# The first stage of a two-layer streaming encoder: x loaded ahead of all else, its squares summed on TensorE, and the order of TensorE's work written down

## The chip, the cores and the metric

The kernel runs on one core of a Trainium2 chip. The metric is the device time of one execution in microseconds (us). TensorE (PE in the profile, its weight loads PEld), VectorE (DVE), ScalarE (ACT) and GpSimd (POOL) compute; SyncE (SP) and ACT issue the transfers from memory, each in its own queue and in order.

## The reference, cut to what matters

x has 256 tokens of 2048 features in 32-bit floats. Layer 0 mixes over time, layer 1 attends; each has an MLP behind it. Only the start of layer 0 changes:

```
mod = c @ w_ada[0] + b_ada[0];  sh1, sc1 = the first two of its six parts
h  = x * rsqrt(mean(x*x) + eps) * g_mix * (1 + sc1) + sh1
xx = shift(h, one token) - h
xr, xw, xk, xv, xa, xg = h + xx * mu[0..5]
v  = xv @ w_v
tanh(xw @ w1), xa @ a1, sigmoid(xg @ g1)      # narrow projections ("lora")
r  = xr @ w_r;   k = xk @ w_k                 # next stage
```

## The kernel before, in words

Features lie on the 128 partitions, so x is 16 K tiles (KT) of 128 features by 256 tokens, held in the tile `h`. Big matrix products are made from two halves of each number: ACT rounds the weights or activations to a short type (`wH`, the H of `aHL`), DVE subtracts to get the rest (`wL`, the L of `aHL`), and TensorE runs three matmuls for each block. The small products, marked fp32 in the source by plain tiles, take two matmul records each in the trace.

The first stage is `layer_a`, up to `s3.close()`. It goes over the 16 K tiles, n = 0 to 15. For each n it needs

- the modulation of these 128 features. `w_ada0` holds, for each n, four blocks of 512 KB (tile name `rawa`, six buffers); 32 matmuls with a 32-column weight (`crep`, c copied over 32 columns) make the products in four column groups of the array (line 631 before; "products" below), ACT copies them to `adat` (637), 8 matmuls with one column sum and turn them (641; "vectors" below), DVE adds the bias (646) and makes the gain (648);
- the norm `r`, from the sum over all 16 tiles of the squares of x: before, ACT squares a tile (485, 488), DVE adds it to `ss` (489), one matmul with ones sums over partitions (494), and DVE and ACT make the reciprocal root (496 to 504);
- h (705 on DVE, 707 on ACT), xx (663, POOL), and five mixes (668, DVE);
- two matmuls and two more for the narrow projections (714, 718, weights `lw`), 24 for the first half of v (722 to 724, weights `raw` from `w_v_rows`), and from n = 4 on 24 for a part of v's second half (`v_part`, 687 to 689, weights `raw` from `w_v`, result in the PSUM tile `t`).

A scheduler sets the order of each engine's instructions from the order of the source and its own estimates; `tc.issue_after(instruction)` keeps what stands in it behind that instruction in the schedule. Tiles from pools with few buffers, and the semaphores of the transfers (eight, used in turn), add waits on SP. Before, the generator `ada_blocks` issues the products of tile n+1 in two halves ahead of tile n's work (`next(adab)` in the loop), and nothing is pinned, so the scheduler puts these matmuls in pieces between others. The transfers of x are split: quarters 1 and 3 on SP ahead of `rawa`, quarters 0 and 2 on ACT behind the first constants.

After `layer_a`'s loop come four more `v_part`, then the projections and the recurrence of layer 0 and all the rest, which the change does not touch.

Of the kernel before, what the change touches and what calls it, by code (L numbers as in the profile page):

```python
# [11 lines left out]
F32 = mybir.dt.float32  # L12
# [5 lines left out]
P = 128  # L18
D = 2048
T = 256  # L20
# [306 lines left out]
class Body:  # L327
# [163 lines left out]
    def rstd(self):  # L491
        nc = self.nc
        ps = self.psm()[:, :T]
        nc.tensor.matmul(ps, self.cst("ones"), self.ss, start=True, stop=True)
# [96 lines left out]
    def layer_a(self, st, sp):  # L591
# [6 lines left out]
        with ExitStack() as s1:  # L598
# [20 lines left out]
            def ada_blocks():  # L619

                for lo in range(KT):
                    ps = self.psm().rearrange("p (i n) -> p i n", i=4)
                    for part in (1, 0):
                        raws = []
                        for a in range(KT // HK):
                            raw = pb.tile([P, HK, P], F32, tag="rawa", bufs=6, name="rawa")
                            nc.sync.dma_start(out=raw, in_=d["w_ada0"][lo, part, a])
                            raws.append(raw)
                        for kt in range(KT):
                            g = 32 * (kt % 4)  # L630
                            nc.tensor.matmul(ps[g:g + 32, part, :], crep[:, kt, :], raws[kt // HK][:, kt % HK, :],
                                             start=(part == 1 and kt < 4), stop=(part == 0 and kt >= KT - 4),
                                             tile_position=(0, g))
                        if part:
                            yield
                    t = pb.tile([P, 2, P], F32, tag="adat", bufs=1, name="adat")
                    nc.scalar.copy(t, ps[:, 0:2, :])
                    ps = self.psm()
                    for part in range(2):
                        for g in range(0, P, 32):  # L640
                            nc.tensor.matmul(ps[g:g + 32, part:part + 1], t[:, part, g:g + 32], self.col(C_32ND),
                                             start=True, stop=True, tile_position=(0, g))
                    o = slice(lo, lo + 1)
                    for part in (1, 0):
                        bias = self.ada_src(0, part)[1]
                        nc.vector.tensor_tensor(out=self.mods[(0, part)][:, o], in0=ps[:, part:part + 1],
                                                in1=bias[:, o], op=ALU.add)
                    nc.vector.scalar_tensor_tensor(out=gain[:, o], in0=self.mods[(0, 1)][:, o], scalar=1.0,
                                                   in1=self.vec("g_mix0")[:, o], op0=ALU.add, op1=ALU.mult)
                    yield  # L650
# [489 lines left out]
```

## Time and profile before

| what | before |
|---|---|
| time, median of 3 runs | 2738.26 us (2733.71 to 2740.51) |
| the profiled execution: time, span | 2732.68 us, 2730.7 us |
| mean granted clock of TensorE | 0.991 |
| busy in the span: PE, DVE, ACT, POOL | 97%, 75%, 50%, 13% |
| first h (705) starts | 26.90 us |
| last h (705) starts | 182.14 us |
| first matmul of the next stage (pj, 400) | 205.86 us |
| moved in the whole span | 662.70 MB, mean 243 GB/s |

The span runs from the first to the last instruction of the profiled execution; its own time is 1.98 us longer. In the answers of the trace each row has a start and a length in us, the engine, the source line, the operation, result <- operands, shape and count, and in brackets the idle time ahead of it and what ended it. A row with a count covers instructions that follow each other. In rows by stretches of time, each engine's busy us stand with the number of instructions, then the granted clock (PEclk, 1.00 is full), the busy share of the 16 DMA engines and GB/s.

### The profile page before, as it was taken

To read this page: it belongs to the slowest core of one execution; us is meant where nothing else is said; L and a number is where in the kernel's file an instruction comes from. 1 tells how busy PE (TensorE), PEld (TensorE's weight loads), DVE (VectorE), ACT (ScalarE), POOL (GpSimd) and SP (SyncE) were. 2 spreads that over 40 slices of the span, in tenths; PEclk is the share of its full clock that TensorE was granted. 3 is DMA by queue.
4 is the path that set the end of the run, shared out by engine and by line. 5 is a ranking of instruction groups with operands and counts; after the bars stand their busy time and mean duration, and the time that the engine had idled before them with its cause. 6 is when DMAs were issued, how large, how long until landed. Compare 5 with 4: busy or idle time off the path is not lost.

```text
span 2730.7 us, 59448 instructions
## 1 busy us (share of the span) xinstructions
PE 2645.1 (97%) x24298; PEld 2250.2 (82%) x24298; DVE 2041.8 (75%) x2986; ACT 1363.3 (50%) x2457; POOL 361.0 (13%) x480
## 2 busy tenths in 40 slices
PE   6999999999999999999999899999999999999997
PEld 5787777777889888888888888877888888888886
DVE  5568777878799687788888788899996655566554
ACT  3346555555457543345544474465465533455443
POOL 0003434443212000000000130000120000000011
PEclk9999999999999999999999999999999999999999
DMA  9866546555688688888888778988875555555553
GB/s 349 299 243 197 172 157 191 191 170 167 214 301 286 224 284 302 316 315 315 308 307 309 249 241 310 329 307 279 283 267 194 185 190 188 187 190 186 190 188 124
DMA packets 192817, 662.70 MB, mean 243 GB/s; under 512 B 21409, under 2 KB 36129, under 8 KB 192545
## 3 DMA queue, kind: packets, MB, share of 16 engines
q1 hardware_dynamic: 190480, 656.36, 70.3%
q8 instruction: 191, 3.13, 0.5%
q10 hardware_dynamic: 2064, 2.54, 0.3%
q14 instruction: 82, 0.66, 0.1%
HBM read 656.72 MB, written 2.10 MB: 241 GB/s over the span
## 4 chain that ended last, share of the span: by engine, by line
PE 77%; DVE 7%; DMA 5%; issue 2%; ACT 2%; POOL 1%; DVEq 0%; SPq 0%; POOLq 0%; ACTq 0%
PE pj L400 41%; PE pj L401 20%; DMA rawt<-w_ada 3%; DVE wL L369 2%; PE iv L106 2%; DVE acc L430 2%; PE gr L100 1%; PE pj L391 1%; PE pj L390 1%; PE pj L389 1%; PE o L389 1%; DMA rawm<-w_ada 1%; ACT wH L366 1%; PE ms L100 1%; PE chn L279 1%
## 5 line engine op out<-in xcount | busy, mean ns | idle before, releaser
L400 PE MATMUL pj<-aHL,wH 128*128 128x512 f32 x4352 | 1574.7, 402 | 4.0 <-DVE ks L962 1.2
L369 DVE TENSOR_TENSOR wL<-raw,wH 128x1024 fp32r<-128x1024 f32 x772 | 951.5, 1234 | 421.7 <-ACT wH L366 419.1
L366 ACT CAST wH<-raw 128x1024 fp32r<-128x1024 f32 x772 | 805.9, 1046 | 878.3 <-PE pj L400 767.5
L401 PE MATMUL pj<-aHL,wL 128*128 128x256 f32 x4352 | 1226.6, 282 | 4.8 <-DVE wL L369 4.4
L400 PEld LDWEIGHTS pj<-aHL,wH 128*128 128x128 f32 x4352 | 821.2, 189 | 203.0 <-issue 11.5
L401 PEld LDWEIGHTS pj<-aHL,wL 128*128 128x128 f32 x4352 | 822.5, 189 | 12.0 <-DVE wL L369 9.5
L400 PE MATMUL pj<-hHL,wH 128*128 128x512 f32 x1024 | 359.0, 394 | 0.0
L401 PE MATMUL pj<-hHL,wL 128*128 128x256 f32 x1024 | 284.2, 278 | 0.0
L489 POOL TENSOR_TENSOR ss<-ss,sq 128x256 f32<-128x256 f32 x56 | 55.2, 986 | 1477.3 <-ACT sq L488 1477.1
L400 PEld LDWEIGHTS pj<-hHL,wH 128*128 128x128 f32 x1024 | 192.0, 188 | 44.5
L430 DVE SCALAR_TENSOR_TENSOR acc<-rawm,ct,acc 128x1024 f32<-128x1024 f32 x165 | 215.3, 1305 | 10.5 <-DMA rawm<-w_ada_kv 6.3
L401 PEld LDWEIGHTS pj<-hHL,wL 128*128 128x128 f32 x1024 | 192.3, 188 | 0.0
L430 DVE SCALAR_TENSOR_TENSOR acc<-rawt,ct,acc 128x1024 f32<-128x1024 f32 x100 | 129.7, 1297 | 21.4 <-DMA rawt<-w_ada 21.1
L430 DVE SCALAR_TENSOR_TENSOR acc<-raw,ct,acc 128x1024 f32<-128x1024 f32 x95 | 127.4, 1341 | 0.8 <-DMA raw<-w_ada 0.6
L389 PE MATMUL pj<-aHL,wH 128*128 128x258 f32 x384 | 112.4, 293 | 9.4 <-DVE ks L976 7.1
L391 PE MATMUL pj<-aHL,wL 128*128 128x258 f32 x384 | 111.4, 290 | 5.6 <-DVE wL L369 5.5
L390 PE MATMUL pj<-aHL,wH 128*128 128x258 f32 x384 | 111.7, 291 | 2.4 <-DVE aHL L513 2.4
L926 DVE SCALAR_TENSOR_TENSOR x<-pj,mod,x 128x256 f32<-128x256 f32 x128 | 61.7, 482 | 38.9 <-PE pj L401 37.2
L519 POOL TENSOR_TENSOR sq<-x,rstd 128x256 f32<-128x256 f32 x64 | 67.7, 1070 | 125.1 <-DVE aHL L522 70.7
L389 PEld LDWEIGHTS pj<-aHL,wH 128*128 128x128 f32 x384 | 75.1, 195 | 10.7 <-issue 7.3
L391 PEld LDWEIGHTS pj<-aHL,wL 128*128 128x128 f32 x384 | 75.9, 198 | 7.0 <-DVE wL L369 6.5
L390 PEld LDWEIGHTS pj<-aHL,wH 128*128 128x128 f32 x384 | 75.3, 196 | 3.0 <-DVE aHL L513 2.8
(255 smaller groups left out, 3026.6 us busy)
## 6 DMA issues: line engine op xcount, KB each, us to landing
raw<-w_up SPq DMA_DIRECT2D x256, 512.0 KB, 4.3
raw<-w_down SPq DMA_DIRECT2D x256, 512.0 KB, 3.9
rawm<-w_ada SPq DMA_DIRECT2D x111, 512.0 KB, 6.0
rawt<-w_ada SPq DMA_DIRECT2D x107, 512.0 KB, 4.7
raw<-w_ada SPq DMA_DIRECT2D x102, 512.0 KB, 4.2
rawa<-w_ada SPq DMA_DIRECT2D x64, 512.0 KB, 6.5
rawm<-w_ada_kv SPq DMA_DIRECT2D x64, 512.0 KB, 6.5
raw<-w_k SPq DMA_DIRECT2D x32, 512.0 KB, 4.0
```

The lines of the kernel that those rows point to most:

```text
L100: self.b.nc.tensor.matmul(o(c)[K], lhsT(c)[K], rhs(c)[K], start=True, stop=True)
L366: nc.scalar.copy(Hf, raw)
L369: eng.tensor_tensor(out=Lf, in0=raw, in1=Hf, op=ALU.subtract)
L389: nc.tensor.matmul(ps, H[:, i, :], a(kt)[:, 0, :], start=(first and kt == 0), stop=False)
L390: nc.tensor.matmul(ps, H[:, i, :], a(kt)[:, 1, :], start=False, stop=False)
L391: ins = nc.tensor.matmul(ps, L[:, i, :], a(kt)[:, 0, :], start=False, stop=(last and kt == KT - 1))
L400: nc.tensor.matmul(ps, H[:, i, :], a(kt), start=(first and kt == 0), stop=False)
L401: ins = nc.tensor.matmul(ps[:, 0, :], L[:, i, :], a(kt)[:, 0, :], start=False, stop=(last and kt == KT - 1))
L430: nc.vector.scalar_tensor_tensor(out=acc, in0=raw, scalar=ck, in1=acc, op0=ALU.mult, op1=ALU.add)
L489: (eng or nc.gpsimd).tensor_tensor(out=self.ss, in0=self.ss, in1=sq, op=ALU.add)
L519: nc.gpsimd.tensor_tensor(out=t, in0=self.x[:, n, :], in1=rstd, op=ALU.mult)
L926: nc.vector.scalar_tensor_tensor(out=x, in0=ps[:, i, :], scalar=self.mods[(layer, 5)][:, n:n + 1], in1=x, op0=ALU.mult, op1=ALU.add)
```

## The change

- The four quarters of x are all issued by SP, ahead of everything else. The constants' second part is no longer loaded at the start by ACT but by SP in the loop's second tile. There the name `first`, which held the column 133 where this part begins, has been set anew in the tile before (`first, last = n == 0, n == KT - 1`); the slice begins at column 1 and takes 1092 columns instead of 960, 546 KB instead of 480. It writes again the ones and the column of 1/32, which the vectors' matmuls read.
- The squares go alternately to ACT and DVE into four buffers (`sqa`), and each is summed by a matmul with ones into one PSUM tile: 16 such matmuls instead of 15 additions and one matmul.
- `ada_blocks` becomes `ada_load`, `ada_products` and `ada_vectors`. In tile n the products of tile n+1 come first, as one group; then the narrow projections; then the first half of v's 24 matmuls; then the vectors of tile n+1; then the second half; then `v_part`. Each of these is kept behind the last matmul issued before it (`behind()`).
- xx of the first two tiles moves from POOL to DVE.

```diff
+            for q in range(4):
+                nc.sync.dma_start(out=h[:, 4 * q:4 * q + 4, 1:T + 1], in_=d["x"][:, 4 * q:4 * q + 4, :])
             nc.scalar.dma_start(out=self.csts[:, :first], in_=d["cst"][:, :first])
-            for q in range(4):
-                (nc.sync if q % 2 else nc.scalar).dma_start(out=h[:, 4 * q:4 * q + 4, 1:T + 1],
-                                                            in_=d["x"][:, 4 * q:4 * q + 4, :])
             nc.scalar.dma_start(out=self.bada, in_=d["b_ada"])
             nc.scalar.dma_start(out=self.vecs, in_=d["vecs"])
-            nc.scalar.dma_start(out=self.csts[:, first:], in_=d["cst"][:, first:])
...
-            def ada_blocks():
...
-            adab = ada_blocks()
-            self.ss_reset()
+            def ada_load(m):
...
+                        nc.sync.dma_start(out=raw, in_=d["w_ada0"][m, part, a])
+            def ada_products(m):
+                raws = ada_load(m) if m else raws0
+                ps = self.psm().rearrange("p (i n) -> p i n", i=4)
+                for part in (1, 0):
+                    for kt in range(KT):
+                        g = 32 * (kt % 4)
+                        nc.tensor.matmul(ps[g:g + 32, part, :], crep[:, kt, :], raws[part, kt // HK][:, kt % HK, :],
...
+                nc.scalar.copy(t, ps[:, 0:2, :])
+                return ps[:, 2, :], t
+            def ada_vectors(m, sums):
...
+            raws0 = ada_load(0)
+            pss = pp.tile([P, 2, T], F32, tag="t", bufs=1, name="t")[:, 0, :]
             for n in range(KT):
-                self.ss_add(h[:, n, 1:T + 1], n, nc.vector)
-            adab_at = 2
-            for i in range(adab_at):
-                next(adab)
-            r = self.rstd()
+                sq, x = pb.tile([P, T], F32, tag="sqa", bufs=4, name="sqa"), h[:, n, 1:T + 1]
+                if n % 2:
+                    nc.vector.tensor_tensor(out=sq, in0=x, in1=x, op=ALU.mult)
+                else:
+                    nc.scalar.activation(sq, x, AF.Square)
+                nc.tensor.matmul(pss, self.cst("ones"), sq, start=(n == 0), stop=(n == KT - 1))
+            ada_vectors(0, ada_products(0))
+            r = self.rstd(pss)
             def diff(n):
-                nc.gpsimd.tensor_tensor(out=xx, in0=h[:, n, 0:T], in1=h[:, n, 1:T + 1], op=ALU.subtract)
+                (nc.gpsimd if n > 1 else nc.vector).tensor_tensor(out=xx, in0=h[:, n, 0:T], in1=h[:, n, 1:T + 1],
+                                                                  op=ALU.subtract)
+            def behind():
+                return tc.issue_after(self.last_pe())
...
             for n in range(KT):
...
-                while adab_at < min(2 * KT, 2 * n + 4):
-                    next(adab)
-                    adab_at += 1
+                if n == 1:
+                    nc.sync.dma_start(out=self.csts[:, first:], in_=d["cst"][:, first:])
+                if n + 1 < KT:
+                    with behind():
+                        sums = ada_products(n + 1)
...
+                with behind():
...                                    # the four matmuls of the narrow projections
+                for half in range(2):
+                    with behind():
+                        for i in range(4 * half, 4 * half + 4):
...                                    # three matmuls of v for each i
+                    if half == 0 and n + 1 < KT:
+                        with behind():
+                            ada_vectors(n + 1, sums)
                 if n == 3:
                     self.v_next = v_part_weight(0)
                 if n >= 4:
-                    v_part(n // 4 - 1, n % 4)
+                    with behind():
+                        v_part(n // 4 - 1, n % 4)
```

What this does to the order, at four places.

TensorE in a tile of the second half of the loop, before (m is the tile of products, v_229 to v_232 the first half of v, l_234 a narrow projection, t is `v_part`):

```order
L714 MATMUL l_233<-mix,lw_2101 96x256 x2
L631 MATMUL m<-rawa,crep 32x128 x8
L722 MATMUL v_229<-aHL,wH 128x256
...
L631 MATMUL m<-rawa,crep 32x128 x8
L718 MATMUL l_234<-mix,lw_2101 128x256 x2
L724 MATMUL v_229<-aHL,wL 128x256
L631 MATMUL m<-rawa,crep 32x128 x8
```

and now, with the last matmul of `v_part` of the tile before in its first row:

```order
L697 MATMUL t<-aHL,wL 128x256
L632 MATMUL m<-rawa,crep 32x128 x32
L725 MATMUL l_231<-mix,lw_1522 96x256 x2
L729 MATMUL l_232<-mix,lw_1522 128x256 x2
L735 MATMUL v_227<-aHL,wH 128x256
```

The 32 products stood in four pieces of 8 between other matmuls; they now stand in one row, ahead of the tile's other work.

SP's queue from the start, before:

```order
L609 DMA h<-x 128x4x256 x2
L627 DMA rawa<-w_ada 128x1024 x4
L699 DMA lw_235<-lora 128x448
L356 DMA raw<-w_v_rows 128x1024
L627 DMA rawa<-w_ada 128x1024 x4
```

and now:

```order
L609 DMA h<-x 128x4x256 x4
L623 DMA rawa<-w_ada 128x1024 x4
L707 DMA lw_233<-lora 128x448
L356 DMA raw<-w_v_rows 128x1024
L623 DMA rawa<-w_ada 128x1024 x4
```

All of x now stands ahead of the first modulation block; the rest is as it was. Further on, where the loop's second tile loads the four blocks for tile 2, SP's row is now, with the semaphores that each waits for:

```order
L623 DMA rawa<-w_ada 128x1024 [waits DMAHW6_49,PE_49]
L710 DMA csts<-cst 128x1092 [waits DMAHW7_49,PE_49]
L623 DMA rawa<-w_ada 128x1024 [waits DMAHW0_49]
L707 DMA lw_452<-lora 128x448 [waits DMAHW1_49]
L356 DMA raw<-w_v_rows 128x1024 [waits DMAHW2_49]
```

The constants have come in ahead of the fourth block for tile 2. Their wait for TensorE (PE_49) ends at its 112th matmul: 16 with ones, 32 products and 8 vectors of tile 0, 32 products of tile 1, 4 of the narrow projections, 12 of v and, last, the 8 vectors of tile 1.

ACT at the start, before:

```order
L609 DMA h<-x 128x4x256 x2
L611 DMA bada<-b_ada 128x224
L612 DMA vecs<-vecs 128x304
L613 DMA csts<-cst 128x960
L485 ACTIVATE ss<-h 128x256
L488 ACTIVATE sq<-h 128x256 x10
L637 COPY adat<-m 128x256
L488 ACTIVATE sq<-h 128x256 x4
L366 CAST wH<-raw 128x1024
L488 ACTIVATE sq<-h 128x256
L498 ACTIVATE rstd<-rv 128x256
```

and now:

```order
L611 DMA bada<-b_ada 128x224
L612 DMA vecs<-vecs 128x304
L660 ACTIVATE sqa<-h 128x256 x8
L499 ACTIVATE rstd<-rv 128x256
L500 ACTIVATE rstd<-rstd 128x256
L636 COPY adat<-m 128x256
L366 CAST wH<-raw 128x1024
```

The copy of the first modulation products and the first rounding of weights stood among the squares; both now stand behind the norm. Past the end of this stage the engines' rows are the same before and now.

More of the change, by code (lines that the diff above doesn't have):

```diff
@@ L489, in ss_add, with rstd @@
             (eng or nc.gpsimd).tensor_tensor(out=self.ss, in0=self.ss, in1=sq, op=ALU.add)
-    def rstd(self):
+    def rstd(self, ps=None):
         nc = self.nc
-        ps = self.psm()[:, :T]
-        nc.tensor.matmul(ps, self.cst("ones"), self.ss, start=True, stop=True)
+        if ps is None:
+            ps = self.psm()[:, :T]
+            nc.tensor.matmul(ps, self.cst("ones"), self.ss, start=True, stop=True)
         v = self.np.tile([P, T], F32, tag="rv", bufs=1, name="rv")
@@ L617, in layer_a @@
             gain = self.gp.tile([P, KT], F32, name="gain_g_mix0")
-            def ada_blocks():
[L621 to L650, printed above, removed]
@@ L652, in layer_a @@
-            adab = ada_blocks()
-            self.ss_reset()
-            for n in range(KT):
-                self.ss_add(h[:, n, 1:T + 1], n, nc.vector)
-            adab_at = 2
-            for i in range(adab_at):
-                next(adab)
-            r = self.rstd()
+            def ada_load(m):
+                raws = {}
+                for part in (1, 0):
+                    for a in range(KT // HK):
+                        raw = raws[part, a] = pb.tile([P, HK, P], F32, tag="rawa", bufs=6, name="rawa")
+                        nc.sync.dma_start(out=raw, in_=d["w_ada0"][m, part, a])
+                return raws
@@ new lines, in ada_products @@
+            def ada_products(m):
+                raws = ada_load(m) if m else raws0
+                ps = self.psm().rearrange("p (i n) -> p i n", i=4)
+                for part in (1, 0):
+                    for kt in range(KT):
+                        g = 32 * (kt % 4)
+                        nc.tensor.matmul(ps[g:g + 32, part, :], crep[:, kt, :], raws[part, kt // HK][:, kt % HK, :],
+                                         start=(part == 1 and kt < 4), stop=(part == 0 and kt >= KT - 4),
+                                         tile_position=(0, g))
+                t = pb.tile([P, 2, P], F32, tag="adat", bufs=1, name="adat")
+                nc.scalar.copy(t, ps[:, 0:2, :])
+                return ps[:, 2, :], t
@@ new lines, in ada_vectors @@
+            def ada_vectors(m, sums):
+                ps, t = sums
+                for part in range(2):
+                    for g in range(0, P, 32):
+                        nc.tensor.matmul(ps[g:g + 32, part:part + 1], t[:, part, g:g + 32], self.col(C_32ND),
+                                         start=True, stop=True, tile_position=(0, g))
+                o = slice(m, m + 1)
+                for part in (1, 0):
+                    bias = self.ada_src(0, part)[1]
+                    nc.vector.tensor_tensor(out=self.mods[(0, part)][:, o], in0=ps[:, part:part + 1],
+                                            in1=bias[:, o], op=ALU.add)
+                nc.vector.scalar_tensor_tensor(out=gain[:, o], in0=self.mods[(0, 1)][:, o], scalar=1.0,
+                                               in1=self.vec("g_mix0")[:, o], op0=ALU.add, op1=ALU.mult)
```

23 lines of the change are left out of this document (11 added, 12 removed).

## The prediction

> **What bounds the kernel now.** I read the page's table of busy time first, then the stretches of the first stage, then its rows in order of time.
>
> ```profile
> PE 2645.1 (97%) x24298; PEld 2250.2 (82%) x24298; DVE 2041.8 (75%) x2986; ACT 1363.3 (50%) x2457; POOL 361.0 (13%) x480
> 0.00:8.40 8.40, 0.00 (x0) 0.00 (x0) 0.50 (x2) 1.28 (x1) 0.21 (x4) 1.00 0.76 268
> 8.40:26.90 18.50, 8.50 (x146) 5.62 (x146) 9.62 (x25) 7.94 (x20) 0.00 (x0) 1.00 1.04 397
> 114.00:182.14 68.14, 67.07 (x818) 54.05 (x818) 41.85 (x91) 21.49 (x37) 5.52 (x6) 1.00 0.80 289
> ```
>
> TensorE is the bound, so only idle or ill-used TensorE time can be won. Until 26.90 us it is busy 8.50 of 18.50 us while transfers run full (1.04, 397 GB/s): a start that waits for x, the norm and the first modulation. Later it is busy 67.07 of 68.14 us, which does not say how well. The start in order of time:
>
> ```profile
> 8.43 1.08 PE L631 MATMUL m<-rawa,crep 128*32 128x128 f32 x16 [8.43 <-DMA rawa<-w_ada]
> 10.77 0.42 ACT L485 ACTIVATE ss<-h 128x256 f32<-128x256 f32 x1 [8.73 <-DMA h<-x]
> 11.09 4.49 ACT L488 ACTIVATE sq<-h 128x256 f32<-128x256 f32 x10
> 16.80 1.08 PE L631 MATMUL m<-rawa,crep 128*32 128x128 f32 x16 [2.89 <-DMA rawa<-w_ada]
> 17.95 0.37 ACT L637 COPY adat<-m 128x256 f32<-128x256 f32 x1 [2.37 <-PE m L631]
> 19.75 1.03 ACT L366 CAST wH<-raw 128x1024 fp32r<-128x1024 f32 x1
> 22.03 0.42 DVE L489 TENSOR_TENSOR ss<-ss,sq 128x256 f32<-128x256 f32 x1
> 22.59 1.19 PE L494 MATMUL m<-ss,csts 128*128 128x256 f32 x2 [3.83 <-DVE ss L489]
> 23.83 0.42 DVE L496 TENSOR_SCALAR rv<-m 128x256 f32<-128x256 f32 x1 [1.38 <-PE m L494]
> 24.31 2.76 PE L631 MATMUL m<-rawa,crep 128*32 128x128 f32 x64 [0.52 <-DVE rv L496]
> 26.90 0.49 DVE L705 SCALAR_TENSOR_TENSOR h<-h,gain_g_mix,rstd 128x256 f32<-128x256 f32 x1
> 28.24 0.31 PE L641 MATMUL m<-csts,adat 128*32 128x1 f32 x16 [1.17 <-ACT adat L637]
> 29.72 2.02 PE L714 MATMUL l<-mix,lw 128*96 128x256 f32 x4 [1.18 <-DVE mix L668]
> ```
>
> The first square waits for x until 10.77. After eleven, ACT stands at the copy of the modulation products, which came with the fourth `rawa` at 16.80, and later rounds weights at 19.75; so the last addition ends at 22.45 and h starts at 26.90.
>
> **The start.** Removed: 15 additions and those two waits in ACT's row. Added: 15 matmuls with ones. Moved: two quarters of x from ACT's queue to SP's, ahead of the modulation blocks.
>
> ```profile
> rawa<-w_ada SPq DMA_DIRECT2D x14, 512.0 KB, 7.0
> raw<-w_v_rows SPq DMA_DIRECT2D x3, 512.0 KB, 6.6
> h<-x SPq DMA_DIRECT2D x2, 512.0 KB, 4.8
> h<-x ACTq DMA_DIRECT2D x2, 512.0 KB, 10.1
> lw<-lora SPq DMA_DIRECT2D x3, 224.0 KB, 6.2
> vecs<-vecs ACTq DMA_DIRECT2D x1, 152.0 KB, 9.0
> bada<-b_ada ACTq DMA_DIRECT2D x1, 112.0 KB, 8.9
> csts<-cst ACTq DMA_DIRECT2D x1, 66.5 KB, 5.2
> 29.50:30.00 0.50, 0.28 (x1) 0.28 (x2) 0.50 (x3) 0.08 (x1) 0.00 (x0) 0.50 1.02 372
> 33.00:34.00 1.00, 1.00 (x9) 0.97 (x9) 0.67 (x1) 0.00 (x0) 1.00 (x1) 1.00 1.02 414
> 36.02 1.95 PE L631 MATMUL m<-rawa,crep 128*32 128x128 f32 x64
> 37.90 1.10 PE L714 MATMUL l<-mix,lw 128*96 128x256 f32 x4
> ```
>
> x (2.10 MB) and the small loads beside it (0.34 MB) are 2.44 MB. Before, the first `rawa` was there at 8.43 behind two quarters of x and with as much again on ACT's queue, so I put that amount at 9 us. The squares (0.42 us each, on two engines) end at about 10 and hold nothing up. The ones landed 5.2 us after an early issue on ACT's queue: about 6.4 us. From there 16 matmuls run one behind another. The same kind of product took 2.02/2 = 1.01 us at a granted clock of 0.50, and 1.10/2 = 0.55, or 0.52 from start to start, at 1.00; between 29.5 and 33 the clock needed about 3.4 us to rise. Bounds: all slow, 16.2 us, end at 22.6; all fast, 8.3, end at 14.7. I take 3.4 us slow (3.3 matmuls) and 12.7 x 0.52 = 6.6: 16.4, or 17 with some waiting for x. From the old sum's end (23.78) to h took 3.1 us: 20.1. Beside it the products of tile 0 follow the ones on TensorE (1.88 us, 36.02 to 37.90), then copy, vectors, bias, gain, about 1.5 us: 20.4. So h starts at about 20.5, **6.4 us** earlier (4 to 9).
>
> [...]
>
> Tile 0's narrow projections also wait for the products of tile 1, now pinned ahead of them. Bytes up to these: 2.44 + 2.10 + 0.75 + 2.10 = 7.39 MB. Before, 8.40 x 0.268 + 18.50 x 0.397 = 9.6 MB were through at 26.90; at 0.397 MB a us 7.39 are there at 21.4, and the products end at about 23. The mixes (h, ACT, a `wL` of 1.2 us, xx, three mixes) are ready at about 24: line 714 starts at 24 instead of 29.72. xx on DVE costs 0.42 us there and saves the hop to POOL; I cost it at nothing, since `rawa` is nearly as late; without that cover it is under 1 us in two tiles.
>
> **Tiles 1 to 4.** The constants are a new wait in SP's row: they are issued after the vectors of tile 1, at 24 + 2.1 + 1.5 = 27.6, and behind them stand the fourth block for tile 2 and all later loads. Without that, TensorE would set these tiles: 7.4 us each (below). With it, 1.08 MB land 2.7 us later at the least (by rate) and 7.0 at most (the `rawa` row); I take 4.8 (x on SP's empty queue): 32.4, products done at 33. From there transfers set the pace: 4 x 0.52 + 0.52 + 0.23 = 2.85 MB a tile, 7.2 us at 397 GB/s; with the first `raw` of `v_part`, 3.37 MB, 8.5 us. Line 714 of tile 4 then starts at 33 + 7.2 + 7.2 + 8.5 = 56, against 59.96 (row below): **4.0 us** left of the start (6 if TensorE alone sets these tiles, -1 if the waits let the clock fall, rival A).
>
> **Tiles 4 to 15.** The steady tile, some rows in order:
>
> ```profile
> 56.90 0.49 DVE L705 SCALAR_TENSOR_TENSOR h<-h,gain_g_mix,rstd 128x256 f32<-128x256 f32 x1
> 182.14 0.48 DVE L705 SCALAR_TENSOR_TENSOR h<-h,gain_g_mix,rstd 128x256 f32<-128x256 f32 x1
> 59.96 1.10 PE L714 MATMUL l<-mix,lw 128*96 128x256 f32 x4 [0.29 <-DVE mix L668]
> 151.03 1.10 PE L714 MATMUL l<-mix,lw 128*96 128x256 f32 x4
> 152.07 0.65 PE L631 MATMUL m<-rawa,crep 128*32 128x128 f32 x16
> 152.64 0.39 PE L722 MATMUL v<-aHL,wH 128*128 128x256 f32 x1
> 152.87 0.29 PE L723 MATMUL v<-aHL,wH 128*128 128x256 f32 x1
> 153.59 0.28 PE L723 MATMUL v<-aHL,wH 128*128 128x256 f32 x1
> 153.80 0.64 PE L631 MATMUL m<-rawa,crep 128*32 128x128 f32 x16
> 158.64 0.31 PE L641 MATMUL m<-csts,adat 128*32 128x1 f32 x16
> 162.47 0.67 PE l L714 x2
> ```
>
> (182.14 - 56.90)/11 = 11.39 us a tile. v matmuls follow each other after 0.12 us (six steps from 152.87 to 153.59), but the first behind a piece of products holds 0.23, and a piece starts 0.21 after the last v: each visit to the column groups costs 0.1 + 0.1 us beside its own 0.57 (152.07 to 152.64). Four pieces and the vectors: 4 x 0.57 + 0.24 + 5 x 0.2 = 3.5 us; narrow projections 4 x 0.52 = 2.1; v and `v_part` 48 x 0.119 = 5.7; sum 11.3, nearly the period. Now: products 1.88, vectors 0.24, two visits 0.4, and 2.1 + 5.7: **10.3 us** (7.4 without `v_part`). Bounds: only the shorter group, 0.4 us a tile won; or 1.3, with the wait of 0.29 ahead of 714 gone too. 11 x 1.05 = **11.5 us** (4 to 14).
>
> What is late next: from the vectors to the next narrow projections 162.47 - 158.64 = 3.83 us, and up to 2 more where a `wL` and an `aHL` come between the mixes. Behind the vectors TensorE now has 1.5 (v) + 2.9 (`v_part`) + 2.1 (products) = 6.5 us: cover by 0.7. The last tile has no products: 0.7 us lost. A tile's 3.37 MB need 8.5 us, under 10.3.
>
> **Sum:** 4.0 + 11.5 - 0.7 = 14.8 us off the profiled execution's 2732.68: 2717.9. The median of runs lies 5.6 above that execution: 2738.26 - 14.8 = 2723.5. Nothing behind the stage is reordered, so I carry the gain to the end whole.
>
> **The rivals.**
>
> A. Cold tiles. In tiles 1 to 4 TensorE waits for blocks with everything else pinned behind them. After the pause between 27.07 (24.31 + 2.76) and 29.72, with 0.31 us of work in it, the clock stood at 0.50 for 3.4 us and lost 1.7. Three such tiles lose 5: gain 9.7, 2728.6; four, 8. Against it: the waits should be about 1 us, not 2.7. [...]
>
> B. The chain of mixes binds. If DVE or ACT are so late that the cover of 0.7 us and the gain of 1 us a tile are gone, the period stays at 11.3: gain 4, 2734. For it: POOL's hop and two roundings in the chain; against: DVE's 41.85 busy of 68.14 us.
>
> C. Slower. Pinned products make every tile wait for transfers. The steady rate was 289 GB/s; were that the most that these issues give, a tile's 3.37 MB took 11.7 us, and at 270 GB/s 12.5: 11 x 1.1 = 12 us lost against 4 won, 2746. It decides below 290. Against it: 397 GB/s at the start, and a DMA share of only 0.80.
>
> **How the numbers follow.** Forecast 0.68, A 0.15, B 0.12, C 0.05. Under 0.3% (8.2 us) this kernel's time can't be told from no change. The forecast and two thirds of A are faster by more: 0.78; the rest of A, B and a little of C 0.18; C 0.04. The range takes in A and goes to 2732, short of B; at the other end stand the better bounds of tiles 1 to 4 and of the period, 6 + 14 - 0.7 = 19, or 2719, and the lower runs' distance to the median (2738.26 - 2733.71, 4 us): 2715.
>
> **What the profile would show.** Ones from about 6.4 to 17 us, halving in length on the way; h at 20 to 21; the first narrow projection at 24; the constants issued at about 28 and a pause of SP ahead of them; tile 4's narrow projections at 56; then 10.3 us a tile with 64 products in one row of 1.9 us; the next stage's first matmul at about 191. Wrong if steady products wait for `rawa`, if the clock falls below 1.00 after 25 us, if narrow projections wait for mixes in each tile, or if later stages give the gain back.

## The result and the profile after

The changed kernel takes 2724.03 us (median of 8 executions, 2715.83 to 2731.16), the kernel before 2737.45 beside it (8 executions, 2733.71 to 2740.51): ratio 0.9949, 95% interval 0.9933 to 0.9965. The profiled execution took 2723.07 us, its span is 2721.3 at a mean granted clock of 0.987 (before: 2730.7 at 0.991).

First the page's table of busy time, then stretches of the first stage (columns as before), cut at the first h (19.02), the first narrow projection (24.41) and that of tile 1 (36.55), and six steady tiles from the narrow projections of tile 4 on (59.09 to 118.55):

```profile
PE 2647.0 (97%) x24328; PEld 2265.5 (83%) x24328; DVE 2040.2 (75%) x2981; ACT 1362.1 (50%) x2449; POOL 353.2 (13%) x478
4.97:19.02 14.05, 11.71 (x116) 9.64 (x120) 5.91 (x18) 5.38 (x12) 0.00 (x0) 1.00 1.05 393
19.02:24.41 5.39, 3.32 (x65) 1.88 (x65) 5.22 (x11) 1.32 (x3) 0.00 (x0) 0.70 1.03 402
24.41:36.55 12.14, 8.93 (x117) 7.31 (x113) 5.75 (x14) 2.74 (x5) 0.00 (x0) 0.85 0.70 256
59.09:118.55 59.46, 59.46 (x820) 54.82 (x817) 40.65 (x89) 24.31 (x40) 3.69 (x6) 1.00 0.98 364
```

The table of busy time hardly moves; the stretches do. Transfers run full until 24.41, then drop to 256 GB/s while TensorE is busy 8.93 of 12.14 us at a clock of 0.85: there the constants hold SP up. (The first row's clock reads 1.00, but the pace of the ones, shown further down, shows that their first 4.6 us ran at half the speed of the rest.) The start in order of time (TensorE, DVE, SP):

```profile
6.20 9.46 PE L661 MATMUL t<-sqa,csts 128*128 128x256 f32 x32 [6.20 <-DMA csts<-cst]
15.58 1.95 PE L632 MATMUL m<-rawa,crep 128*32 128x128 f32 x64
19.02 0.49 DVE L715 SCALAR_TENSOR_TENSOR h<-h,gain_g_mix,rstd 128x256 f32<-128x256 f32 x1
22.10 1.08 PE L632 MATMUL m<-rawa,crep 128*32 128x128 f32 x16 [1.50 <-DMA rawa<-w_ada]
24.41 2.02 PE L725 MATMUL l<-mix,lw 128*96 128x256 f32 x4
18.14 1.84 SPq L623 DMA_DIRECT2D rawa<-w_ada  x3
29.80 0.33 SPq L710 DMA_DIRECT2D csts<-cst  x1
35.97 0.65 PE L632 MATMUL m<-rawa,crep 128*32 128x128 f32 x16 [3.21 <-DMA rawa<-w_ada]
59.09 1.10 PE L725 MATMUL l<-mix,lw 128*96 128x256 f32 x4
```

The first h comes 7.9 us earlier than before (26.90), the first narrow projection 5.3 (29.72), but tile 4's only 0.9 (59.96): between them stand the 9.8 us in which SP issues nothing, from 19.98 (18.14 + 1.84) to 29.80, and TensorE's wait of 3.21 us for a block issued behind the constants.

The steady tile, the last tile and the next stage:

```profile
63.18 0.49 DVE L715 SCALAR_TENSOR_TENSOR h<-h,gain_g_mix,rstd 128x256 f32<-128x256 f32 x1
108.60 1.10 PE L725 MATMUL l<-mix,lw 128*96 128x256 f32 x4
...
110.22 0.47 PE L735 MATMUL v<-aHL,wH 128*128 128x256 f32 x1
116.67 1.95 PE L632 MATMUL m<-rawa,crep 128*32 128x128 f32 x64
118.55 1.10 PE L725 MATMUL l<-mix,lw 128*96 128x256 f32 x4
162.39 0.48 DVE L715 SCALAR_TENSOR_TENSOR h<-h,gain_g_mix,rstd 128x256 f32<-128x256 f32 x1
185.61 0.40 PE L400 MATMUL pj<-aHL,wH 128*128 128x512 f32 x1
```

(162.39 - 63.18)/10 = 9.92 us a tile instead of 11.39, and nothing waits. The next stage begins at 185.61 instead of 205.86: the stage has won 20.25 us. The span is only 9.4 us shorter, and the medians lie 13.4 apart. So some of the stage's gain is lost behind it, where the change touches nothing. In the same places of the two programs the gain is 18.9 us at about 500 us, 14.4 at 620, 9.2 at 745, and 7.4 to 9.5 from there on. Two places take nearly all of that, 5.1 us at 584 and 5.3 at 702 (half of each half-clock stretch, and at the second a pause of 1.9 that the profile of the kernel before does not have). This is the first, by stretches of time, in the kernel before, in the changed one, and in a second profile of the changed one (`again`, below):

```profile
599.46:602.87 3.41, 1.95 (x11) 1.28 (x9) 3.41 (x4) 1.46 (x3) 3.41 (x3) 1.00 0.56 166
603.50:613.50 10.00, 9.91 (x123) 7.95 (x123) 6.67 (x15) 6.59 (x21) 3.02 (x9) 1.00 0.51 167
```
```profile
580.91:584.32 3.41, 1.86 (x11) 1.24 (x9) 3.41 (x5) 1.38 (x3) 3.41 (x3) 1.00 0.54 169
584.30:594.50 10.20, 9.55 (x68) 7.32 (x69) 3.72 (x9) 3.27 (x12) 3.58 (x9) 0.50 0.31 98
```
```profile
588.03:591.44 3.41, 1.97 (x22) 1.75 (x24) 1.36 (x3) 1.39 (x4) 3.01 (x6) 1.00 0.74 214
589.50:599.50 10.00, 10.00 (x125) 8.03 (x127) 6.79 (x15) 6.70 (x21) 2.88 (x8) 1.00 0.51 162
```

In each, TensorE stands idle at the same step of the recurrence. In the changed kernel's first profile the clock then stands at 0.50 for 10.2 us and 68 matmuls run where 123 run at 1.00. The idle time is the same in the three, as TensorE's rows show (kernel before, changed kernel, `again`):

```profile
603.59 0.39 PE L123 MATMUL py<-sL,bones 128*128 128x256 f32 x1 [2.18 <-POOL sL L118]
```
```profile
584.95 0.58 PE L123 MATMUL py<-sL,bones 128*128 128x256 f32 x1 [2.17 <-POOL sL L118]
```
```profile
589.47 0.39 PE L123 MATMUL py<-sL,bones 128*128 128x256 f32 x1 [2.18 <-POOL sL L118]
```

So the same pause of 2.2 us is followed by half clock in one execution and not in another of the same program. In the traces the stretches at 0.50 last 3.4, 6.8 or 10.2 us nearly everywhere (a few 13.7, as in `sl_dve` from 224.6 to 238.3), and within each of the 13 profiles here all changes of the clock lie on one grid with a step of 3.413 us: up to 2680 us 12 changes in the profile of the kernel before and 18 in the first of the changed one, each within 0.001 us of its grid.

The grid also tells the executions apart. The first rows of the three pairs above are each a step of their own profile's grid, the one with the larger part of the pause: TensorE is idle for 1.46 us of it before, 1.55 in the changed kernel (3.41 - 1.86) and 1.44 in `again`, and only the second is followed by half clock. Over the 13 profiles, between 150 and 2680 us, a step at full clock with 1.5 us or more of idle TensorE is followed by half clock in 74 of 77 cases, one with 1.4 to 1.5 in 8 of 22, and one with 0.9 to 1.4 in 3 of 100; in the profile of the kernel before and the first of the changed one alone it is 13 of 14, none of 3 and none of 15. So what follows a pause of this length goes here with how it lies on the grid, as far as a count over traces can show it; no run moved a pause to test it.

### The profile page after: what moved, and what is told of

Read it like the earlier page. It is cut to its first block, busy times and chain, and to the rows that moved or that the text cites. A ratio compares the mean times of both kernels' runs of the same rounds, so it can differ in the third digit from the quotient of the medians.

```text
span 2721.3 us, 59484 instructions
## 1 busy us (share of the span) xinstructions
PE 2647.0 (97%) x24328; PEld 2265.5 (83%) x24328; DVE 2040.2 (75%) x2981; ACT 1362.1 (50%) x2449; POOL 353.2 (13%) x478
## 3 DMA queue, kind: packets, MB, share of 16 engines
q8 instruction: 191, 3.13, 0.5%
## 4 chain that ended last, share of the span: by engine, by line
PE 80%; DVE 8%; DMA 7%; issue 2%; ACT 2%; POOL 1%; SPq 0%; DVEq 0%; ACTq 0%; POOLq 0%
PE pj L400 40%; PE pj L401 20%; DVE wL L369 3%; DMA rawt<-w_ada 2%; PE iv L106 2%; DVE acc L430 2%; PE gr L100 1%; PE pj L391 1%; PE pj L389 1%; PE pj L390 1%; DMA rawa<-w_ada 1%; PE m L632 1%; DMA raw<-w_q 1%; PE o L389 1%; ACT wH L366 1%
## 5 line engine op out<-in xcount | busy, mean ns | idle before, releaser
L400 PEld LDWEIGHTS pj<-aHL,wH 128*128 128x128 f32 x4352 | 821.9, 189 | 201.1 <-issue 10.1
L389 PE MATMUL pj<-aHL,wH 128*128 128x258 f32 x384 | 112.8, 294 | 10.2 <-DVE ks L993 7.3
L389 PEld LDWEIGHTS pj<-aHL,wH 128*128 128x128 f32 x384 | 75.4, 196 | 11.5 <-issue 7.7
```

What stands on the lines that cost most here:

```text
L389: nc.tensor.matmul(ps, H[:, i, :], a(kt)[:, 0, :], start=(first and kt == 0), stop=False)
L400: nc.tensor.matmul(ps, H[:, i, :], a(kt), start=(first and kt == 0), stop=False)
```

## Experiments

In each table, h, first and tile 4 are the starts of the first h and of the narrow projections of tiles 0 and 4, pj is the next stage's first matmul, all in us from the profile.

**The same kernel once more, and the late constants put right** (`again`, `csts960`). The second slices the constants from column 133, so that it writes nothing that TensorE reads.

```diff
-                    nc.sync.dma_start(out=self.csts[:, first:], in_=d["cst"][:, first:])
+                    nc.sync.dma_start(out=self.csts[:, CST_AT["ident"][0]:], in_=d["cst"][:, CST_AT["ident"][0]:])
```

> The changed kernel once more, nothing edited. In its first profile the first stage ended 19 us earlier, but 10 us of that were lost between 580 and 715 us, where the granted clock fell to 0.50 twice after a pause of TensorE of about 2 us that the kernel before has too, without the fall. Theory 1: whether the clock falls at such a pause is chance, not the change. Then the falls come at other pauses this time, or at none, and the span less half of the time at 0.50 stays at 2721.3 - 73.9/2 = 2684 +-3 us. Theory 2: the change's own timing brings the falls about. Then they are at the same two places (after the pauses at 582.8 and 702.0 us), and the gain at 700 us is again about 9 us against the kernel before.

> The late constants are read from column 133 on (960 columns), so that nothing that TensorE reads is written again, and SP's row has no wait for TensorE there. Theory: the pause of 3.2 us ahead of the last products for tile 2 (32.8 us) goes; SP issues the constants at about 19 instead of 29.8 us, tile 4's narrow projections start at 55 to 56 instead of 59.09 us, and the last h at 159 instead of 162.39; 3 us won. Rival: the transfers of tiles 1 to 4 are the limit anyway, tile 4 starts at 58 to 59 us, and under 1 us is won.

**The two halves of the change apart** (`order_only`, `start_only`). The first keeps the pinned order, but x on two queues, the constants on ACT at the start, the sum by ACT and DVE, and xx on POOL, as before. The second is the kernel before with x first on SP and the sum of squares on TensorE.

```diff
             for q in range(4):
-                nc.sync.dma_start(out=h[:, 4 * q:4 * q + 4, 1:T + 1], in_=d["x"][:, 4 * q:4 * q + 4, :])
+                (nc.sync if q % 2 else nc.scalar).dma_start(out=h[:, 4 * q:4 * q + 4, 1:T + 1],
+                                                            in_=d["x"][:, 4 * q:4 * q + 4, :])
...
-                nc.tensor.matmul(pss, self.cst("ones"), sq, start=(n == 0), stop=(n == KT - 1))
+                self.ss_add(h[:, n, 1:T + 1], n, nc.vector)
```

> The order of TensorE's work as in the changed kernel, but the start as before: x split over two queues, squares by ACT and added by DVE, constants at the start by ACT, xx on POOL. Theory: the order alone is worth (11.39 - 9.92) x 11 = 16 us from tile 4 to 15: a period of 9.9 us, and the last h at about 166 us against 182.14 before; 2721 by the kernel before's median of 2737.5, if later stages keep it. Rival: without the early start the first tiles are later, the pinned products wait for transfers, and no more than 10 us are won by the last h (172 or later).

> The start as in the changed kernel (x first on SP, squares summed by TensorE, xx still on POOL, constants by SP's neighbour ACT at the start), with the order of the rest left to the scheduler as before. Theory: the first narrow projections start 5 us earlier (24 to 25 us instead of 29.72) and this is carried through: last h at 177, 2732 by the kernel before's median. Rival: tiles 1 to 4 wait for transfers, tile 4's narrow projections stay at about 59 us, and the start is worth under 2 us by the last h (180 or later).

These four ran on one chip, the kernel before beside them at 2734.82 (18 executions):

| kernel | median (executions) | ratio, 95% interval | first | tile 4 | pj |
|---|---|---|---|---|---|
| again | 2723.36 (10) | 0.9959, 0.9944 to 0.9975 | 24.46 | 61.51 | 188.36 |
| csts960 | 2716.01 (5) | 0.9926, 0.9905 to 0.9947 | 24.47 | 54.94 | 181.69 |
| order_only | 2722.80 (5) | 0.9957, 0.9942 to 0.9972 | 29.69 | 60.58 | 188.16 |
| start_only | 2745.74 (8) | 1.0049, 1.0032 to 1.0066 | 23.55 | 61.20 | 206.00 |

The second profile of the changed kernel has no fall of the clock behind the pause near 588 us, but others elsewhere, one of them in the stage itself: at 35.1 us, in the wait behind the constants, which is why tile 4 comes 2.4 us later. So the falls are not bound to the change's two places (theory 2), but the sum that theory 1 named was not met either: the span less half of the time at 0.50 is 2688 us, not 2684 +-3.

In `csts960` SP's row does not stop, and the block that came at 35.97 is there when TensorE wants it:

```profile
17.94 0.43 SPq L710 DMA_DIRECT2D csts<-cst  x1
31.03 1.95 PE L632 MATMUL m<-rawa,crep 128*32 128x128 f32 x64
```

The constants are issued 11.9 us earlier, and tile 4 comes 4.15 us earlier than in the change. That is the price of the wait; 3.9 of it are left at pj. The median lies 7.35 us under that of `again`, but five executions from 2711.93 to 2730.15 do not tell how much of that is the edit's.

In `order_only` the start is that of the kernel before, and pj still comes 17.7 us earlier than 205.86: nearly all of the 20.25 belongs to the order. The new start adds 2.5 (188.16 to 185.61), and 6.5 without the wait for the constants (181.69). `start_only` has its first narrow projection 6.2 us earlier than before and nothing of it left at tile 4. Its TensorE in tiles 3 and 4:

```profile
50.82 0.67 PE L719 MATMUL l<-mix,lw 128*96 128x256 f32 x2 [1.39 <-DVE mix L673]
61.20 1.10 PE L719 MATMUL l<-mix,lw 128*96 128x256 f32 x4 [0.31 <-DVE mix L673]
```

Without the pinned order TensorE runs out of ready work and waits for the mixes. That is not all of the loss: between its first narrow projection and that of tile 4 it is idle for 3.6 us (0.3 before), and it does 4.1 us of matmuls (busy 34.1 us against 29.9) that the kernel before had done ahead of its first narrow projection. The rival, no gain from the start alone, was right in its outcome; its reason, waits for transfers, is not what the rows show. The median is even worse than before: its profile shows the stage no longer than before (206.00 against 205.86), and behind it half-clock stretches of 6.8 us at 442.6 and 13.7 us at 722.5 that the kernel before's profile lacks, each behind a pause of TensorE that no other engine ends (1.99 and 1.52 us; more on these at the end of the next section). By the mean of all executions it loses 35 us to half clock, (1 - clock) x span, where the kernel before beside it loses 26; the 4 us more that it takes are of the size of these two pauses, which is not proof.

**Who sums the squares** (`dve_sum`). x stays first on SP and the order pinned; ACT squares and DVE adds, with one matmul with ones, as before.

```diff
-                sq, x = pb.tile([P, T], F32, tag="sqa", bufs=4, name="sqa"), h[:, n, 1:T + 1]
...
-                nc.tensor.matmul(pss, self.cst("ones"), sq, start=(n == 0), stop=(n == KT - 1))
+                self.ss_add(h[:, n, 1:T + 1], n, nc.vector)
             ada_vectors(0, ada_products(0))
-            r = self.rstd(pss)
+            r = self.rstd()
```

> The changed kernel with x first on SP, but the squares all by ACT, summed by DVE and one matmul with ones, as before; the pinned order is kept. Theory: x's place in the queues makes the earlier start, and TensorE's sum is no quicker than DVE's 15 additions of 0.42 us, since its 16 matmuls took 9.46 us, the first of them at half clock, and the products of tile 0 stand behind them. Then the first h starts at 18.5 to 20.5 us (19.02 with TensorE's sum), the first narrow projection at 24 to 25, the next stage at 185 to 187, and the time is that of the changed kernel within 0.2%. Rival: TensorE's sum is what is won; then the first h starts at 22 to 24, the first narrow projection at 26 to 27, and the next stage some 2 us later than 185.61.

Measured: 2718.05 us (4 executions), ratio 0.9938 (0.9919 to 0.9956) to the kernel before at 2736.71; h at 21.89, first 24.35, tile 4 57.77, pj 185.33.

```profile
10.06 3.60 DVE L489 TENSOR_TENSOR ss<-ss,sq 128x256 f32<-128x256 f32 x7
18.01 0.67 PE L495 MATMUL m<-ss,csts 128*128 128x256 f32 x2 [0.50 <-DVE gain_g_mix L650]
21.89 0.49 DVE L710 SCALAR_TENSOR_TENSOR h<-h,gain_g_mix,rstd 128x256 f32<-128x256 f32 x1
22.67 1.03 PE L632 MATMUL m<-rawa,crep 128*32 128x128 f32 x16 [0.23 <-DMA rawa<-w_ada]
24.35 0.89 PE L720 MATMUL l<-mix,lw 128*96 128x256 f32 x3 [0.65 <-DVE mix L671]
```

The last products of tile 1 and their block, in the change:

```profile
23.40 1.08 PE L632 MATMUL m<-rawa,crep 128*32 128x128 f32 x16 [0.21 <-DMA rawa<-w_ada]
```

On h the rival was nearly right (22 to 24), on the rest the theory. DVE's sum ends at 13.66, before TensorE's (15.66), but its one matmul stands in TensorE's row behind the products and vectors of tile 0, and starts at 18.01. So h is 2.9 us late, and TensorE waits 0.65 us for a mix ahead of the first narrow projection, which it does not in the change. That this starts at 24.35 all the same is two differences that cancel: with no ones ahead of them the products of tile 0 start at 11.88 us instead of 15.58, SP has issued the four blocks for tile 1 by 14.5 instead of 17.1, and the last of them is used from 22.67 on, 0.7 us earlier. Where the norm's matmul stands in TensorE's row and when the blocks land matters; which engine adds makes no difference here that the first narrow projection or pj would show.

**What a visit to the column groups costs** (`twice_joined`, `twice_apart`). Both issue the eight vectors' matmuls of each tile a second time, into the same place. The first does it right behind the first copy, the second in a place of its own between two groups of v's matmuls.

```diff
+                    if half == 2 and n + 1 < KT:
+                        with behind():
+                            sum_up(sums)
```

> The changed kernel with the eight vectors' matmuls of each tile issued twice, the second time right behind the first. Both theories expect 8 x 0.03 us more in a tile: the steady period goes from 9.92 to about 10.15 us. It is there for the comparison with the next kernel.

> As the one before, with the same matmuls, but the second copy stands in a place of its own, between two groups of v's matmuls, so that TensorE goes to the column groups once more in each tile. Theory (each visit costs about 0.2 us, the reading on which the period of the prediction rests): the period is 0.2 us above that of the kernel before, about 10.35. Rival (a visit costs nothing, and the shorter period comes from something else, such as the projections' own matmuls or the waits ahead of them): the same period within 0.05 us. By the period of 9.92 itself, 0.4 below the 10.3 of the prediction, a visit could also cost about 0.3.

Narrow projections of tile 4 and, ten tiles on, of tile 14; joined, then apart:

```profile
58.28 1.10 PE L729 MATMUL l<-mix,lw 128*96 128x256 f32 x4
158.76 1.10 PE L729 MATMUL l<-mix,lw 128*96 128x256 f32 x4
```
```profile
59.95 0.89 PE L729 MATMUL l<-mix,lw 128*96 128x256 f32 x3
163.48 0.89 PE L729 MATMUL l<-mix,lw 128*96 128x256 f32 x3
```

The periods are 10.05 and 10.35 us (one execution each, 2721.44 and 2719.14 us; executions of one program differ by more than that). The second copy itself costs 0.13 us, and the place of its own 0.30: about 0.2 in the gaps beside it, as the prediction had read, and 0.1 in the group itself, which takes 0.24 apart and 0.13 joined. The theory's 10.35 is met only because the joined kernel came 0.10 under its forecast. So a visit has a price here, and 0.30 us is its size.

**The pauses behind the stage** (`sl_dve`, `before_sl`, `after_sl`). In the recurrence, TensorE waits for sL, a difference that POOL makes for the sums of py. One call of it goes to DVE: in `sl_dve` on top of the mended constants, in the two others on the kernel before and on the change as it is.

```diff
-        nc.gpsimd.tensor_tensor(out=L, in0=src, in1=H, op=ALU.subtract)
+        (eng or nc.gpsimd).tensor_tensor(out=L, in0=src, in1=H, op=ALU.subtract)
...
-        sq = self.parts(AF.Square, py)
+        sq = self.parts(AF.Square, py, eng=nc.vector)
```

> The changed kernel with two edits: the late constants start at column 133 again, and in the recurrence the subtraction that makes sL for the sums of py (line 118, for this one call) goes from POOL, where it took 1.70 us behind another of 1.70, to DVE. Theory (the falls of the clock between 200 and 850 us follow TensorE's pauses of about 2 us, four or five of them at py, line 123, waiting for sL): these pauses shrink below 1 us, no fall follows them, the half-clock time in that stretch is 10 to 20 us instead of 20 to 54, and the median is 5 to 10 us below the 2716.01 of the kernel with the constants alone, 2706 to 2711. Rival (falls come whatever pauses there are, or DVE, now later with its own work, makes new pauses in the same place): half-clock time and median as there, 2713 to 2719.

> The kernel before, with one edit outside the first stage: the subtraction that makes sL for the sums of py goes from POOL to DVE. It shows what that edit alone is worth, and is the base for the next kernel. Theory (the pauses at py cost their own length of about 1.7 us, five times, and now and then a fall of the clock behind them): 8 to 13 us below the kernel before, ratio 0.9952 to 0.9971, with half-clock time of 40 to 50 us a run against the 52 that 25 runs of the kernel before had in the mean. Rival (it only helped where the change had moved the recurrence to another moment): within 0.15% of the kernel before.

> The changed kernel with that edit alone (the late constants as in the change). Against the kernel before_sl on the same chip it shows what the change is worth where the pauses at py are gone from both. Theory (the stage wins 18 to 20 us up to the next stage's first matmul, and what the medians of before and after lack of that, 13.4 instead of 20, went to falls of the clock behind the pauses of the recurrence): 17 to 21 us below before_sl, a median of 2707 to 2711. Rival (the gain is lost for another reason, such as waits further on that only the changed kernel has): 9 to 14 us below before_sl, as the change was below the kernel before; 2712 to 2717.

| kernel | median (executions) | the kernel before beside it | ratio, 95% interval |
|---|---|---|---|
| sl_dve | 2706.45 (4) | 2736.71 | 0.9893, 0.9869 to 0.9917 |
| before_sl | 2727.05 (6) | 2737.18 | 0.9956, 0.9940 to 0.9972 |
| after_sl | 2709.22 (5) | 2737.18 | 0.9896, 0.9881 to 0.9911 |

Some of TensorE's longest waits between 200 and 850 us (sum, times, longest), in the changed kernel and in `sl_dve`, and the edited operation in `sl_dve`:

```profile
PE py L123 <- POOL sL L118: 7.6, 4, 2.2
PE py L292 <- issue: 1.9, 1, 1.9
```
```profile
PE iv L106 <- DVE tt L238: 4.1, 4, 2.1
```
```profile
L118 DVE TENSOR_TENSOR sL<-pt,sH x16: 412/426/829, 263.4 to 709.1; 128x256 fp32r<-128x256 f32 x16
```

The waits at py are gone, and no half clock stands between 238 and 784 us in that profile; 17.1 us are left between 200 and 850, where `csts960` had 54.6. The waits at iv remain (4.1 us in four, against 4.3 in five in the changed kernel), and 13.7 us at half clock, from 224.6 to 238.3, follow one of them. The times came as the theory said in all three (in `after_sl` by the medians). What the clock alone gave back is less than the two profiles suggest: that of `csts960` is its slowest execution, and the profile of the kernel before, with four pauses at py, has 17.1 us at half clock in this stretch too. By the mean of all executions the time lost to half clock is 22 us in `before_sl` against 29 beside it, 25 in `after_sl` against 33 in the change, and 27 in `sl_dve` against 29 in `csts960`. The edit alone wins 10.1 us without the change (`before_sl`). With the pauses gone from both, the change wins 2727.05 - 2709.22 = 17.8 us by the medians, 16.5 by the means, instead of 13.4; in its profiles the stage wins 20.20 (pj at 206.42 and 186.22). `sl_dve` is the fastest kernel of this study, 17.6 us under the change's 2724.03 (on another chip) and 30.3 under the kernel before beside it.

**The first tile's own work first** (`own_first`). As `sl_dve`, but in tile 0 the products of tile 1 stand behind the narrow projections and half of v.

```diff
+                    if half == 0 and n == 0:
+                        with behind():
+                            sums = ada_products(1, raws1)
```

> The kernel with the constants from column 133 and sL on DVE, and in tile 0 alone the products of tile 1 behind the narrow projections and the first half of v, not ahead of them. Theory (from x's arrival on the first tile waits only for the blocks of tile 1, the last of which came at 23.86, and everything behind is TensorE's own work): the first narrow projection starts at 21.5 to 22.5 us instead of 24.88, TensorE waits for no block, and the narrow projections of tile 1 start at 30.5 to 31.5 instead of 32.71, the next stage 1 to 2 us before 181.55. Rival (the pause from 17.9 us to the first narrow projection, now with no products in it, lets the clock fall for longer, or transfers bind tiles 1 to 4): the narrow projections of tile 1 at 32.3 or later, and the next stage at 181.2 or later.

```profile
22.22 2.02 PE L727 MATMUL l<-mix,lw 128*96 128x256 f32 x4 [3.61 <-DVE mix L676]
26.90 1.95 PE L632 MATMUL m<-rawa,crep 128*32 128x128 f32 x64
31.25 0.48 DVE L717 SCALAR_TENSOR_TENSOR h<-h,gain_g_mix,rstd 128x256 f32<-128x256 f32 x1
33.71 1.10 PE L727 MATMUL l<-mix,lw 128*96 128x256 f32 x4 [0.34 <-DVE mix L676]
```

The first narrow projection comes 2.7 us earlier, tile 1's 1.0 later than in `sl_dve` (32.71), pj at 183.48 instead of 181.55. The rival's outcome, but for neither of its reasons: the half-clock stretch there is shorter (3.4 us instead of 6.8), and no matmul waits for a block. What is late is the vectors of tile 1, now behind products that start at 26.90; h of tile 1 waits for them, at 31.25 instead of 29.77. Pinned ahead, the products of the next tile give the chain of h its lead. (2710.11 us, one execution.)

## Why the prediction was right, point by point

The forecast of 2723.5 us came out at 2724.03. That it lies so near is luck: the stage won 20.25 us where 14.8 was forecast, and part of it was lost behind the stage where nothing was forecast. Most of the stage's gain came in the way that was forecast, by the shorter period.

- **Ones and h.** Ones from 6.20 to 15.66 (6.4 to 16.4 or 17 forecast), h at 19.02 (20.5). ACT, which waits for every second of the ones to free a buffer, shows their pace:

```profile
9.13 0.42 ACT L660 ACTIVATE sqa<-h 128x256 f32<-128x256 f32 x1 [1.29 <-PE t L661]
10.84 0.42 ACT L660 ACTIVATE sqa<-h 128x256 f32<-128x256 f32 x1 [1.29 <-PE t L661]
12.67 0.42 ACT L660 ACTIVATE sqa<-h 128x256 f32<-128x256 f32 x1 [0.45 <-PE t L661]
13.53 0.42 ACT L660 ACTIVATE sqa<-h 128x256 f32<-128x256 f32 x1 [0.45 <-PE t L661]
```

  1.71 us for two, then 0.86: it halves, as forecast, though later (about 4.6 us after the first instead of 3.4) and to 0.43 each instead of 0.52. The 3.4 us were an estimate from one rise of the clock in the kernel before (at 0.50 from 29.43 to 32.84 us); no run shows them for a start, where these 4.6 us stood in their place. That the early start needs x's place in the queues and not TensorE's sum was not seen; `dve_sum` shows it for the first narrow projection and for pj, not for h (24.35 with x first on SP, 29.69 in `order_only` with x on two queues, both with DVE's sum). The move of xx to DVE was not run alone.
- **First narrow projection.** 24.41 (24 forecast), for the reason given: the products of tile 1, released by their blocks (the last from 23.40 on).
- **The constants.** The mechanism was right: SP waits for the vectors of tile 1. Two sizes failed. The issue came at 29.80 instead of 27.6, because the clock fell at 21.1 for 6.8 us while the products waited for blocks, and the narrow projections and the first of v ran at half speed: one of the signs that the prediction had named for being wrong (a clock below 1.00 after 25 us; it lasted to 27.9). From the issue to the block took 6.2 us (29.80 to 35.97) where 4.8 was taken from a range of 2.7 to 7.0. So tile 4 came at 59.09 instead of 56, and the **start term was 0.9 instead of 4.0 us**. From the products to tile 4 took 22.5 us (23 forecast).
- **The period.** 9.92 instead of 10.3 us: the **period term was 16 us instead of 11.5**. The visits were sized well: the working has three of them at 1.0 us in all (3 x 0.2 in the gaps, and four pieces of 0.57 against one of 1.88), `twice_apart` makes it 0.90, and the rows show 0.93 (from each start to the next, in the mean of ten tiles from tile 4 on: products 2.30 before and 1.88 now, v's first half 3.76 and 3.24). The term that failed is the narrow projections: 4 x 0.52 = 2.1 was set for both orders, where they took 1.86 before and 1.62 now (108.60 to 110.22). That the old sum closed at 11.3 all the same was luck, since it had no term for waits, which took 0.31 us a tile, mostly for mixes; they are gone too. 0.93 + 0.24 + 0.31 is the 1.47 us won in a tile.
- **Last tile.** The loss of 0.7 us did not come: behind the last `v_part` TensorE waits 0.17 us for a mix. Instead 3.3 us were won that the sum has no term for. In the new order the products of tile n+1 stand ahead of the narrow projections of tile n, so tile 4's mark lies behind the products of tile 5, and the last step, from tile 14 to 15 (158.30 to 166.24), has none in it: 7.94 us, 2.0 less than a period. These 2.0 are work done before the mark at tile 4, and belong to the start, which by work was worth 2.9 us. The other 1.3 came between tile 15's narrow projections and pj, where a wait of 0.87 us for v is gone. So the stage's gain of 20.25 us is 0.9, 11 x 1.46 = 16.1, and 3.3.
- **"Nothing behind the stage is reordered, so I carry the gain to the end whole."** This step failed, and with it came another of the signs, that later stages give the gain back. By the mean of all executions here whose clock is on record (36 of before, 18 of the change) span times granted clock fell by 17.9 us, 2707.2 to 2689.3, while the time lost to half clock, (1 - clock) x span, rose from 27 to 33 us: 12 us in all. Part of this rise belongs to the stage: 6.8 and 13.6 us at half clock in the two profiles, against 3.4. The rest falls, in the profiles, behind pauses further on, mostly in the recurrence, and with the pauses at py gone the change keeps 16.5 to 17.8 of 20.2 us.
- **Rivals.** A (cold tiles) happened in part: at 21.1 and 21.4 us in the two profiles, and at 35.1 in the second, each in a wait for blocks with all else pinned behind; the second cost 2.4 us at tile 4. B did not (no wait for mixes in steady tiles; without the pinned order, `start_only`, there is one). C did not: from 59.09 to 118.55 us TensorE is never idle, and transfers move 364 GB/s, above the 290 below which C was to decide.

With the pauses at py gone, 2 to 4 us of the stage's gain are still missing at the end. By the mean of the executions they are time at half clock: span times granted clock falls by 19.7 us from `before_sl` to `after_sl`, and the time lost to half clock rises from 22 to 25 us. One more kind of pause stands ahead of such falls, up to about 2 us long, in the middle of a row of small matmuls, and no other engine ends it (`again` and the changed kernel; below them the transfers on queue q8 in the page of the changed kernel: packets, MB, share):

```profile
423.70 0.21 PE L298 MATMUL chn<-sa,bk 64*64 64x64 f32 x1 [2.32 <-issue]
```
```profile
703.88 0.47 PE L292 MATMUL py<-kr,zs 64*64 64x64 f32 x2 [1.89 <-issue]
q8 instruction: 191, 3.13, 0.5%
```

It stands at different places in two executions of one program, a fall of the clock follows it in both, and the kernel before's profile has one of 0.76 us only. The 191 transfers of kind "instruction" on q8 are packets of 16 KB, and their sum, 3.13 MB, divided by TensorE's 24328 matmuls and as many weight loads is 64 bytes for each. In the 13 profiles here 15 of the sixteen "issue" pauses of more than 0.7 us between 60 and 2690 us end 2.3 to 2.5 us after such a packet starts (2.4 at 251.64 us in the kernel before, 2.3 at 703.88 in the changed one), and the sixteenth 3.1 us after one that itself took 0.7 us longer; the pauses that another engine ends have no common distance (in the profiles of these two kernels they end 0.2 to 25 us after the last such packet's start). That TensorE waits there for its own instructions is an estimate from these distances and from that sum, and no run tests it. What brings such a pause about stays open.

## What to carry to other kernels

Group small matmuls that need another shape of the array: here one more return to the column groups in each tile cost 0.30 us (`twice_apart` against `twice_joined`), and writing the order down was worth 17.7 of the stage's 20.25 us, while a start 6 us earlier was worth nothing without it. A transfer put into a loop can wait for the engine that reads what it overwrites, and everything behind it in its queue waits too: SP issued nothing for 9.8 us, and the 132 columns too many cost 4.15 us at tile 4. A gain in one stage can be lost in the stages behind it where TensorE pauses for about 2 us; look for such pauses in the list of waits, since half clock can follow: here 10.2 us of it, a loss of 5.1, behind a pause of 2.17.

## What was not expected of the hardware

- A TensorE pause of 2.17 us was followed by half clock for 10.2 us in one execution of the changed kernel (584.95 us), that of 2.18 us at the same step of the recurrence by none in another (`again`, 589.47). The idle time in one step of the clock's 3.413 us grid was 1.55 us in the first and 1.44 in the second; of the steps at full clock with 1.5 us or more of it, 74 of 77 were followed by half clock in the 13 profiles.
- Span times granted clock varies less between 18 executions of the change (standard deviation 3.0 us) than the times do (4.9 us).
- POOL took between 0.72 and 1.80 us for the same subtraction of 128 x 256 in the recurrence of `sl_dve`; DVE took 0.43 in the median, 0.83 at most.
